# One block of a hybrid encoder on Trainium2: sixteen transfers for the out projection's weight sums, moved and spaced

## The chip, the cores and the metric

The kernel runs on one core of a Trainium2 chip. The metric is device microseconds of one execution, and the time of a kernel is the median over several. A core has five engines that take instructions in order, each from its own queue: TensorE (PE, matmuls; PEld are its weight loads), VectorE (DVE), ScalarE (ACT), GpSimd (POOL) and SyncE (SP, which here only issues transfers). Transfers are issued by SP, POOL and ACT, each on a queue of its own, and carried out by 16 DMA engines that all queues share.

## The reference

One layer of 1024 frames by 1024 channels. A normalised input goes through one projection, and its columns feed three mixers, whose results are gated, projected, summed and sent through an out projection. A gated convolutional feed-forward block follows.

```python
h = _rmsnorm(x, norm_mix_g[l])
z = h @ w_in[l]
(hq, hf, hi, hg, fq, fk, fv, ff, mq, gate_logits) = jnp.split(z, pts, axis=-1)
y_a = _hgrn2_mixer(hq, hf, hi, hg, ...)      # recurrence, 4 heads, 128x128 state, chunkwise
y_b = _fox_mixer(fq, fk, fv, ff, ...)        # forgetting attention, 8 heads of 64, causal
y_c = _memory_mixer(mq, mem_kv, ...)         # attention into 256 memory tokens
gates = jax.nn.sigmoid(gate_logits).reshape(B, T, N_BRANCH, D_MODEL)
merged = (gates[:, :, 0] * (y_a @ w_br_hgrn[l])
          + gates[:, :, 1] * (y_b @ w_br_fox[l])
          + gates[:, :, 2] * (y_c @ w_br_mem[l]))
x = x + merged @ w_out[l]
x = x + _conv_glu_ffn(_rmsnorm(x, norm_ffn_g[l]), w_up, conv_w, conv_b, w_down)
```

The attention works in blocks of 128 queries: logits plus a cumulative log-forget bias, a causal mask, softmax, and the product with the values. `w_out` is 1024 by 1024 in float32.

## The kernel before

Every large product is made of float32 operands split into a rounded part h and a rest l, and costs three matmuls (`mm3`, lines 108 to 112: h by h, h by l, l by h). Large products are also done in seven block products in place of eight (after Strassen and Winograd), for which sums of blocks of both operands are needed. For the out projection the weight sums are made ahead of time, without any compute engine: `out_sums` (lines 922 to 927) is a generator of 16 transfers of 512 KB within DRAM, issued on POOL's queue. Four blocks of the DRAM tile `od` are each first filled by a copy and then added to by an accumulating transfer, each in two halves: od0 is copied from quarter 2 of `w_out`, od1 from quarter 0, od0 is increased by quarter 3, od3 is copied from quarter 1, od1 is increased by od0, od2 is copied from quarter 0, od3 is increased by od1, od2 by quarter 2. `weight_parts` (line 929) is that generator. What it makes is read much later, at the out projection, from 944 us on.

By time the stages are: memory attention, norm and the first projections up to some 330 us; the forgetting attention, some 330 to 700; the recurrence, some 700 to 935; the out projection to some 1060; the feed-forward block to the end.

Attention and recurrence have much less matrix work than they have chains of small steps, so they are woven with other work. `fill` is a generator of steps: the remaining channel-major projections (lines 746 to 870, the tiles `uh`, `ul`, `us`, `ur`, `uo`), and then the three branch projections, whose weights `w_br` come in as chunks `ur` (line 860). `FOX_FILL` and `HGRN_FILL` say how many steps go to each head, and `weave` deals them between the head's own steps. The order of instructions on each engine is then set by a planner, which simulates a timeline and picks by priority (`ahead` gives the mixers' steps more). `tc.issue_after(x)` makes an instruction be queued behind x on its engine. So any edit in these stages can deal the order of all engines anew.

An attention head h (`fox_attn`, line 1014) goes through eight blocks tb of 128 queries. For each block POOL makes the masked bias `nfm` (line 1027); TensorE makes logits from kh and kl, the two parts of the keys (lines 1033, 1034); VectorE adds the bias and takes the maximum; ScalarE takes Exp; POOL normalises `pt` (line 1051). For each pair of blocks TensorE transposes `pt`, ScalarE casts it (`ph`, line 116), and TensorE multiplies by the values `vhl` (lines 1074, 1075, product `po`). The operands of the next head (`fox_load`, lines 999 to 1010: kh, qa and kl in two transfers of 256 KB each, two `nf` of 256 KB, `vhl` of 512 KB) are issued on SP behind the first store `yp` of the head before it.

The recurrence (`hgrn_mix`, line 1122) goes through 4 heads of two halves. Its loads per half are hG, hH, hq, hz and hi. `kE` is transposed (line 1201), copied by ScalarE as `kT` (line 1203) and used at line 1206. `finish` (lines 1101 to 1120) norms a half's result; it is called eight times, and each call takes two transfers from `weight_parts` and queues them on POOL behind its reciprocal root (line 129). `load_y` (line 937) loads a branch operand of 2 MB as `B22l` and `B22h`.

Of the kernel before, what the change touches and what calls it, by code (L numbers as in the profile page):

```python
# [12 lines left out]
ALU = mybir.AluOpType  # L13
AX = mybir.AxisListType

P = 128
# [52 lines left out]
def tile_block(ctx: ExitStack, tc: tile.TileContext, xT, x_rows, memT, mem_rows, vec, fbias, mats, hmask, w_ff, w_tm, w_cm,  # L69
               w_mkv, w_br, w_out, w_up, w_dn, outT):  # L70
    nc = tc.nc
    V, S, G, PE, SP = nc.vector, nc.scalar, nc.gpsimd, nc.tensor, nc.sync
# [7 lines left out]
    def ps_lg():  # L80
        return pz.tile([P, HB], F32, tag="lg", name="lg", bufs=2)

    def ps_tr():
        return pz.tile([P, HB], F32, tag="tr", name="tr", bufs=2)

    def ps_po():
        return pz.tile([P, HB], F32, tag="po", name="po", bufs=1)
# [34 lines left out]
    def split(eng, h, l, src, sub=None):  # L122
        cast(eng, h, src)
        return (sub or V).tensor_sub(l, src, h.bitcast(F32))  # L124

    def rstd_small(out, ss, n):
        w = ss.shape[1]
        V.tensor_scalar(out, ss, 1.0 / n, EPS, ALU.mult, ALU.add)
        return G.tensor_tensor(out, out, mhalf[:, :w], ALU.pow)
# [790 lines left out]
    def out_sums():  # L920

        half = [slice(2 * a, 2 * a + 2) for a in range(2)]
        copy = [(i, w_out[:, a], {}) for i, a in ((0, 2), (1, 0), (3, 1), (2, 0))]
        add = [(i, b, dict(accum_op=ALU.add)) for i, b in ((0, w_out[:, 3]), (1, od[:, 0]), (3, od[:, 1]), (2, w_out[:, 2]))]
        for i, src, how in (copy[0], copy[1], add[0], copy[2], add[1], copy[3], add[2], add[3]):
            for ks in half:
                yield G.dma_start(od[:, i, ks], src[:, ks], **how)

    weight_parts = out_sums()
# [65 lines left out]
    mskf = pf.tile([P, P], F32, tag="mskf", name="mskf")  # L995
# [3 lines left out]
    def fox_load(h):  # L999
        p, a = h // 2, slice(64 * (h % 2), 64 * (h % 2) + 64)  # L1000
        kh, qa, kl = (pf.tile([P, T], F32R, tag=f"{t}{h % 2}", name=f"{t}_{h}") for t in ("kh", "qa", "kl"))
        for t, (u, v) in ((kh, (0, 0)), (qa, (2, 3)), (kl, (1, 1))):
            SP.dma_start(t[0:64, :].bitcast(F32), kqd[p][u // 2][a, u % 2, :])
            SP.dma_start(t[64:128, :].bitcast(F32), kqd[p][v // 2][a, v % 2, :])
        nf = [pf.tile([P, HB], F32, tag="nf", name="nf", bufs=3) for _ in range(2)]
        for n, t in enumerate(nf):
            SP.dma_start(t, negFd[h:h + 1, n * HB:(n + 1) * HB].partition_broadcast(P))
        vhl = pf.tile([P, 8, P], F32R, tag="vhl", name="vhl", bufs=2)
        SP.dma_start(vhl.bitcast(F32), vhd[h // 4][:, :, h % 4, :])
        return kh, kl, qa, vhl, nf  # L1010
# [3 lines left out]
    def fox_attn(h):  # L1014
        p, a = h // 2, slice(64 * (h % 2), 64 * (h % 2) + 64)
        with tc.issue_after(marks["head"].ins) if h else nullcontext():
            kh, kl, qa, vhl, nf = fox_load(h)
        for tp in range(4):
            pts = []
            for j in range(2):  # L1020
                tb = 2 * tp + j
                ns = (tb + 1) * P
                tsl = slice(tb * P, (tb + 1) * P)
                pt = pf.tile([P, T], F32, tag="pt", name="pt", bufs=4)
                st = pf.tile([P, 4], F32, tag="st", name="st", bufs=4)
                nfm = pf.tile([P, P], F32, tag="nfm", name="nfm")
                G.tensor_tensor(nfm, nf[tb // 4][:, tb % 4 * P:tb % 4 * P + P], mskf, ALU.add)
                m = 0
                for s0 in range(0, ns, HB):
                    w = min(HB, ns - s0)  # L1030
                    ps = ps_lg()
                    with tc.issue_after(begun.ins):
                        PE.matmul(ps[:, :w], qa[:, tsl], kh[:, s0:s0 + w], start=True, stop=False)
                    PE.matmul(ps[:, :w], qa[:, tsl], kl[:, s0:s0 + w], start=False, stop=True)

                    d = w - P if s0 + w == ns else w
                    for lo, hi, bias in ((0, d, nf[s0 // HB][:, :d]), (d, w, nfm)):
                        if lo < hi:
                            V.tensor_tensor_reduce(out=pt[:, s0 + lo:s0 + hi], in0=ps[:, lo:hi], in1=bias,
                                                   op0=ALU.add, op1=ALU.max, scale=1.0, scalar=-3e38,  # L1040
                                                   accum_out=st[:, m:m + 1])
                            m += 1
                if m == 3:
                    V.tensor_tensor(st[:, 0:1], st[:, 0:1], st[:, 2:3], ALU.max)
                if m > 1:
                    V.tensor_scalar(st[:, 2:3], st[:, 0:1], st[:, 1:2], -1.0, ALU.max, ALU.mult)  # L1046
                else:
                    V.tensor_scalar(st[:, 2:3], st[:, 0:1], -1.0, None, ALU.mult)
                S.activation(pt[:, :ns], pt[:, :ns], AF.Exp, bias=st[:, 2:3], accum_out=st[:, 3:4])  # L1049
                V.reciprocal(st[:, 3:4], st[:, 3:4])  # L1050
                G.tensor_scalar(pt[:, :ns], pt[:, :ns], st[:, 3:4], 0.0, ALU.mult, ALU.add)  # L1051
                pts.append(pt)
                yield
            po = ps_po()
            for sp in range(tp + 1):
                ptr = ps_tr()
                w = 384 if sp == tp else 512
                for jj in range(2):
                    sb = 2 * sp + jj
                    ssl = slice(sb * P, (sb + 1) * P)  # L1060
                    if sb <= 2 * tp:
                        PE.transpose(ptr[:, jj * 256:jj * 256 + P], pts[0][:, ssl], ident)
                        PE.transpose(ptr[:, jj * 256 + P:jj * 256 + 256], pts[1][:, ssl], ident)
                    else:
                        PE.transpose(ptr[:, 256:384], pts[1][:, ssl], ident)
                ph = pf.tile([P, HB], F32R, tag="ph", name="ph", bufs=2)
                pl = pf.tile([P, HB], F32R, tag="pl", name="pl", bufs=2)
                split(S, ph[:, :w], pl[:, :w], ptr[:, :w])
                for jj in range(2):
                    sb = 2 * sp + jj  # L1070
                    last = sb == 2 * tp + 1
                    o = po[:, P:256] if last else po[:, 0:256]
                    src = slice(256, 384) if last else slice(jj * 256, jj * 256 + 256)
                    PE.matmul(o, vhl[:, sb, :], ph[:, src], start=(sb == 0), stop=False)
                    PE.matmul(o, vhl[:, sb, :], pl[:, src], start=False, stop=last)  # L1075
                yield
            yp = pf.tile([64, 256], F32, tag="yp", name="yp")
            S.copy(yp, po[64:128, :256])
            V.tensor_add(yp, po[0:64, :256], yp)
            stored = SP.dma_start(yd3[1][a, p, tp * 256:(tp + 1) * 256], yp)  # L1080
            if tp == 0:
                marks["head"] = stored
            yield

    for h in range(8):
        weave((ahead(fox_attn(h), AHEAD), FOX_STEPS), (islice(fill, FOX_FILL[h]), FOX_FILL[h]))
# [14 lines left out]
    def finish(h, n, po, gz):  # L1101
        sl = slice(n * HB, (n + 1) * HB)
        o2 = ph.tile([P, 4, P], F32, tag="kE", name="o2", bufs=2)
        rr = ph.tile([P, 4], F32, tag="rr", name="rr", bufs=2)
        S.activation(o2, po.rearrange("p (b v) -> p b v", b=4), AF.Square)
        V.reduce_sum(rr, o2, axis=AX.X)
        marks["last"] = rstd_small(rr, rr, 4 * P)
        with tc.issue_after(marks["last"].ins):
            for _ in range(2):
                next(weight_parts, None)  # L1110
        for b in range(4):
            S.activation(o2[:, b, :], po[:, b * P:(b + 1) * P], AF.Copy, scale=rr[:, b:b + 1])
        ptr = ps_tr()
        for b in range(4):
            PE.transpose(ptr[:, b * P:(b + 1) * P], o2[:, b, :], ident)
        V.scalar_tensor_tensor(out=gz, in0=ptr, scalar=hgc, in1=gz, op0=ALU.mult, op1=ALU.mult)
        if h < 3:
            late.append(partial(SP.dma_start, yd3[0][:, h, sl], gz))
        else:
            y_last.append(gz)  # L1120

    def hgrn_mix(h):
        St = None
        for n in range(2):
# [85 lines left out]
            for b in range(4):  # L1210
# [4 lines left out]
                if n == 0 or b < 3:  # L1215
# [6 lines left out]
                    St = Sn  # L1222

            late.append(partial(finish, h, n, po, gz))
            yield

# [583 lines left out]
```

## Time and profile before

| what | value |
| --- | --- |
| median of 3 runs | 1707.48 us (1705.03 to 1708.06) |
| profiled execution | 1705.12 us |
| its span | 1703.3 us |
| mean granted TensorE clock | 0.995 |
| TensorE busy | 1672.3 us (98%) |
| VectorE busy | 1222.6 us (72%) |
| ScalarE busy | 844.1 us (50%) |
| GpSimd busy | 441.0 us (26%) |
| the 16 transfers of line 927 | issued from 746.4 to 931.1 us |

The span runs from the first to the last event of the profiled execution; the rest of its time lies around it. Busy times leave out the issuing of transfers. A row of the timeline is start, duration, engine, line, operation, output and inputs, sizes, and in brackets how long the engine sat idle before it and what ended that. TensorE's matmuls are pipelined, so each row's duration overlaps the next one's start. A row of waits is the waiting engine, tile and line, what it waited for, then the total, the number of times and the longest, in us.

### The profile page before, as it was taken

How to read it: one execution, taken by the hardware profiler on the slowest of the kernel's cores; microseconds unless marked ns; L12 is line 12 of the kernel's file. 1: busy time of each engine (PE TensorE's matmuls, PEld its weight loads, DVE VectorE, ACT ScalarE, POOL GpSimd, SP SyncE). 2: the span in 40 equal slices, each digit the busy share in tenths (PEclk: the TensorE clock that was granted, in tenths of full speed). 3: DMA queues.
4: the chain of work that ended last, by engine and by line, in shares of the span. 5: the costliest groups of instructions: out<-in, count | busy, mean ns of one | idle time of the engine just before them, and what ended most of it. 6: DMA issues, size and time to landing. Idle time of an engine off the chain costs nothing.

```text
span 1703.3 us, 24929 instructions
## 1 busy us (share of the span) xinstructions
PE 1672.3 (98%) x8883; PEld 1412.6 (83%) x8883; DVE 1222.6 (72%) x2187; ACT 844.1 (50%) x1449; POOL 441.0 (26%) x472
## 2 busy tenths in 40 slices
PE   8999999999999999999999999999999999999999
PEld 5989999777878888888788888888888888788887
DVE  7865766588877666688677768778778777674654
ACT  7745554466656566555333367434444334343331
POOL 1433644565444434222011123211111111100000
PEclk9999999999999999999999999999999999999999
DMA  7353453855545452547756996755345454394772
GB/s 288 111 187 108 162 211 102 256 178 184 187 116 162 146 158 88 185 157 259 265 167 167 273 233 157 226 151 160 117 130 155 130 147 138 139 387 129 263 249 87
DMA packets 133309, 302.92 MB, mean 178 GB/s; under 512 B 14168, under 2 KB 31832, under 8 KB 132544
## 3 DMA queue, kind: packets, MB, share of 16 engines
q1 hardware_dynamic: 101008, 210.87, 36.8%
q0 software_dynamic: 22960, 75.77, 17.6%
q10 hardware_dynamic: 9216, 14.68, 2.4%
q8 instruction: 70, 1.15, 0.3%
q14 instruction: 55, 0.45, 0.1%
HBM read 223.21 MB, written 107.41 MB: 194 GB/s over the span
## 4 chain that ended last, share of the span: by engine, by line
PE 77%; DMA 8%; DVE 7%; issue 4%; ACT 2%; POOL 2%; SPq 1%; DVEq 0%; POOLq 0%; ACTq 0%
PE pp L110 15%; PE pp L112 15%; PE pp L111 15%; PE lg L111 4%; PE lg L112 4%; PE lg L110 4%; PE tr L112 2%; PE tr L110 2%; PE tr L111 2%; DMA hgd<-uo 1%; PE po L110 1%; PE po L112 1%; PE po L1075 1%; PE po L111 1%; DMA fk<-hgd 1%
## 5 line engine op out<-in xcount | busy, mean ns | idle before, releaser
L1349 ACT CAST wh<-s 128x512 fp32r<-128x512 f32 x80 | 48.8, 618 | 119.8 <-PE pp L111 64.8
L116 ACT CAST dwh<-wr 128x1024 fp32r<-128x1024 f32 (+1 forms) x41 | 40.1, 977 | 119.6 <-PE tr L111 40.4
L1349 ACT CAST wh<-rw 128x512 fp32r<-128x512 f32 x70 | 43.0, 620 | 89.3 <-PE pp L111 48.4
L746 ACT CAST uh<-ur 128x512 fp32r<-128x512 f32 x78 | 47.9, 615 | 56.3 <-PE pp L111 40.8
L1472 POOL DMA_DIRECT2D rw<-in_w_up x40 | 22.2, 566 | 199.2 <-DVE wl L1350 162.9
L124 DVE TENSOR_TENSOR dwl<-wr,dwh 128x1024 fp32r<-128x1024 f32 (+1 forms) x41 | 46.3, 1130 | 38.0 <-ACT dwh L116 37.2
L747 DVE TENSOR_TENSOR ul<-us,uh 128x512 fp32r<-128x512 f32 x72 | 55.5, 777 | 24.6 <-ACT uh L746 24.4
L1051 POOL TENSOR_SCALAR pt<-pt,st 128x128 f32<-128x128 f32 (+3 forms) x64 | 56.9, 890 | 56.8 <-DVE st L1050 45.1
L752 POOL TENSOR_TENSOR us<-ur 128x512 f32<-128x512 f32 x36 | 49.0, 1360 | 83.6 <-DMA ur<-in_w_cm 66.6
L747 DVE TENSOR_TENSOR ul<-ur,uh 128x512 fp32r<-128x512 f32 x78 | 61.5, 789 | 12.7 <-ACT uh L746 12.5
L110 PE MATMUL pp<-T2h,uh 128*128 128x512 f32 x168 | 67.3, 403 | 0.2 <-ACT ue L757 0.2
L110 PE MATMUL pp<-B21h,uh 128*128 128x512 f32 x168 | 67.3, 401 | 0.1
L111 PE MATMUL pp<-T2l,uh 128*128 128x512 f32 x168 | 67.0, 399 | 0.0
L112 PE MATMUL pp<-T2h,ul 128*128 128x512 f32 x168 | 66.6, 397 | 0.0
L112 PE MATMUL pp<-B21h,ul 128*128 128x512 f32 x168 | 66.3, 395 | 0.2 <-DVE ul L747 0.2
L111 PE MATMUL pp<-B21l,uh 128*128 128x512 f32 x168 | 66.2, 394 | 0.0
L1049 ACT ACTIVATE pt<-pt,st 128x128 f32<-128x128 f32 (+3 forms) x64 | 49.6, 776 | 30.2 <-DVE st L1046 27.6
L1350 DVE TENSOR_TENSOR wl<-rw,wh 128x512 fp32r<-128x512 f32 x70 | 47.0, 686 | 20.3 <-PE pp L112 16.1
L746 ACT CAST uh<-us 128x512 fp32r<-128x512 f32 x72 | 43.6, 617 | 32.3 <-PE pp L111 21.7
L752 POOL TENSOR_TENSOR us<-us,ur 128x512 f32<-128x512 f32 x36 | 47.6, 1323 | 37.0 <-issue 28.6
L124 DVE TENSOR_TENSOR pl<-tr,ph 128x512 fp32r<-128x512 f32 (+1 forms) x80 | 49.6, 629 | 10.5 <-ACT ph L116 10.0
L1350 DVE TENSOR_TENSOR wl<-s,wh 128x512 fp32r<-128x512 f32 x80 | 54.6, 683 | 0.0
(721 smaller groups left out, 6144.5 us busy)
## 6 DMA issues: line engine op xcount, KB each, us to landing
rw<-in_w_up POOLq DMA_DIRECT2D x40, 512.0 KB, 4.8
ur<-in_w_cm SPq DMA_DIRECT2D x72, 256.0 KB, 3.5
sd<-in_w_dn POOLq DMA_DIRECT2D x30, 512.0 KB, 6.0
br<-yd SPq DMA_DIRECT2D x30, 512.0 KB, 4.3
gd<-uo ACTq DMA_DIRECT2D x48, 256.0 KB, 2.8
gt<-gd SPq DMA_DIRECT2D x48, 256.0 KB, 3.6
yd<-fc SPq DMA_DIRECT2D x44, 256.0 KB, 2.1
raw<-in_w_tm SPq DMA_DIRECT2D x20, 512.0 KB, 4.6
```

The costliest lines, as they stand in the source:

```text
L110: PE.matmul(ps, lh, rh, start=first, stop=False, skip_group_check=more)
L111: PE.matmul(ps, lh, rl, start=False, stop=False, skip_group_check=more)
L112: return PE.matmul(ps, ll, rh, start=False, stop=last, skip_group_check=more)
L116: S.copy(out, in_)
L124: return (sub or V).tensor_sub(l, src, h.bitcast(F32))
L746: marks["cast"] = S.copy(h, src)
L747: V.tensor_sub(l, src, h.bitcast(F32))
L752: G.tensor_add(t, a, b)
L1049: S.activation(pt[:, :ns], pt[:, :ns], AF.Exp, bias=st[:, 2:3], accum_out=st[:, 3:4])
L1051: G.tensor_scalar(pt[:, :ns], pt[:, :ns], st[:, 3:4], 0.0, ALU.mult, ALU.add)
L1349: late["cast"] = S.copy(h, src)
L1350: late["split"] = V.tensor_sub(l, src, h.bitcast(F32))
```

## The change

The sixteen transfers stay as they are and keep their sequence. They are handed out at other places: each of the eight attention heads takes one at block tb = 6, queued on POOL behind that block's masked bias, and each of the eight calls of `finish` takes one in place of two. So the three first steps of the list and the copy of od3 go out in the attention, the rest in the recurrence.

```diff
-                G.tensor_tensor(nfm, nf[tb // 4][:, tb % 4 * P:tb % 4 * P + P], mskf, ALU.add)
+                masked = G.tensor_tensor(nfm, nf[tb // 4][:, tb % 4 * P:tb % 4 * P + P], mskf, ALU.add)
+                if tb == 6:
+                    with tc.issue_after(masked.ins):
+                        next(weight_parts, None)
                 m = 0
...
         marks["last"] = rstd_small(rr, rr, 4 * P)
         with tc.issue_after(marks["last"].ins):
-            for _ in range(2):
-                next(weight_parts, None)
+            next(weight_parts, None)
         for b in range(4):
```

Lines behind the first edit have other numbers in the kernel after: 1051 is 1054 there, 1080 is 1083, and lines 1129 and 1131 are 1131 and 1133. The order of the queues changes from the first attention heads to the end of the recurrence. Three places show it.

On POOL, head 1 around its block 6; `pt` with 768 columns is the softmax of block 5 and with 896 that of block 6. Before:

```order
L1051 TENSOR_SCALAR pt<-pt,st 128x640
L1027 TENSOR_TENSOR nfm<-nf,mskf 128x128
L791 TENSOR_SCALAR uo<-uo 128x512
L792 DMA hgd_80<-uo 128x512
L1051 TENSOR_SCALAR pt<-pt,st 128x768
```

And now:

```order
L1054 TENSOR_SCALAR pt<-pt,st 128x640
L791 TENSOR_SCALAR uo<-uo 128x512
L1027 TENSOR_TENSOR nfm<-nf,mskf 128x128
L927 DMA od<-in_w_out 128x1024
L792 DMA hgd_80<-uo 128x512
L1054 TENSOR_SCALAR pt<-pt,st 128x768
```

The transfer stands behind the bias of block 6, and a store and the normalising of block 5 stand behind the transfer; the clamp of `uo` has moved ahead of the bias.

On SP, around the loads of head 3 (kh_3 to vhl); `fk` and `uo` are results of the projection in the fill that are stored to the recurrence's inputs `hgd3`. Before:

```order
L1009 DMA vhl_4975<-vhd0_74 128x8x128
L966 DMA hgd3_81<-fk_3_6485 128x1024 x2
L812 DMA ur_6868<-in_w_cm 128x512
L1080 DMA yd1_88<-yp_4715 64x256
L799 DMA hgd3_81<-uo_6602 128x512
L799 DMA hgd3_81<-uo_6690 128x512
```

And now:

```order
L966 DMA hgd3_81<-fk_3_6492 128x1024
L812 DMA ur_6876<-in_w_cm 128x512
L1083 DMA yd1_88<-yp_4640 64x256
L1003 DMA kh_3_4965<-kqd1_71 64x1024
...
L1009 DMA vhl_4978<-vhd0_74 128x8x128
L966 DMA hgd3_81<-fk_3_6492 128x1024
L799 DMA hgd3_81<-uo_6609 128x512
L1083 DMA yd1_88<-yp_4717 64x256
L799 DMA hgd3_81<-uo_6697 128x512
```

One of the two stores of `fk` and the load of `ur` have moved from behind the head's loads to ahead of them.

On SP in the recurrence, around the fourth chunk of a branch weight (ur_9553 before, ur_9556 now) and the 2 MB of B22. Before:

```order
L860 DMA ur_9500<-in_w_br 128x512
L888 DMA gt_9392<-gd_86 128x512
L1131 DMA hi_2_9188<-hid1_77 128x4x128
L888 DMA gt_9390<-gd_86 128x512
L1129 DMA hG_3_9587<-hgd3_81 128x512
L1129 DMA hH_3_9588<-hgd3_81 128x512
L888 DMA gt_9498<-gd_86 128x512
L937 DMA B22l_9387<-yd2_89 128x2048
L937 DMA B22h_9386<-yd2_89 128x2048
L1129 DMA hq_3_9589<-hgd3_81 128x512
L860 DMA ur_9553<-in_w_br 128x512
```

And now:

```order
L1133 DMA hi_2_9192<-hid1_77 128x4x128
L860 DMA ur_9556<-in_w_br 128x512
L937 DMA B22l_9390<-yd2_89 128x2048
L937 DMA B22h_9389<-yd2_89 128x2048
L888 DMA gt_9443<-gd_86 128x512
L860 DMA ur_9619<-in_w_br 128x512
L888 DMA gt_9499<-gd_86 128x512
L1131 DMA hG_3_9590<-hgd3_81 128x512
L1131 DMA hH_3_9591<-hgd3_81 128x512
```

The chunk has moved ahead of the 2 MB, and the last head's hG and hH behind them.

## The prediction

> **What bounds the kernel now.** I read the page's busy times first, then windows by stage, then TensorE's waits between 330 and 950 us, then the timeline around the longest of them.
>
> ```profile
> span 1703.3 us, 24929 instructions
> PE 1672.3 (98%) x8883; PEld 1412.6 (83%) x8883; DVE 1222.6 (72%) x2187; ACT 844.1 (50%) x1449; POOL 441.0 (26%) x472
> q1 hardware_dynamic: 101008, 210.87, 36.8%
> q0 software_dynamic: 22960, 75.77, 17.6%
> ...
> 330.00:500.00 170.00, 161.26 (x817) 133.62 (x818) 136.69 (x359) 107.74 (x200) 87.77 (x94) 0.98 0.55 175
> 500.00:700.00 200.00, 200.00 (x1079) 171.03 (x1078) 130.62 (x387) 118.75 (x240) 85.19 (x101) 1.00 0.45 135
> 700.00:950.00 250.00, 245.08 (x1353) 206.18 (x1353) 196.47 (x364) 114.02 (x219) 39.04 (x38) 0.99 0.69 217
> 410.00:420.00 10.00, 6.67 (x27) 5.21 (x26) 6.61 (x18) 5.48 (x10) 4.32 (x5) 0.83 1.03 319
> 470.00:480.00 10.00, 7.15 (x31) 6.05 (x31) 7.91 (x19) 7.39 (x17) 7.34 (x9) 0.83 0.28 85
> 810.00:820.00 10.00, 6.40 (x29) 4.67 (x29) 5.94 (x14) 3.48 (x7) 0.00 (x0) 0.83 1.02 337
> 1100.00:1200.00 100.00, 100.00 (x432) 80.89 (x431) 76.86 (x115) 41.44 (x63) 16.74 (x27) 1.00 0.55 157
> ```
>
> The columns of a window are its length, the busy time of PE, PEld, DVE, ACT and POOL with counts, the granted clock, the DMA share and GB/s. TensorE is busy 98% of the span, so the time is its work plus its gaps. The change touches no matmul and only the stretch from the attention to the end of the recurrence, 330 to 950 us. There TensorE idles 8.7 + 0.0 + 4.9 = 13.7 us. That is all a transfer can give back, besides the slow matmuls behind a gap (the clock of 0.83 in three of the windows). Which waits make it up:
>
> ```profile
> PE tr L1206 <- ACT kT L1203: 3.6, 1, 3.6
> PE lg L1034 <- DMA kl<-kqd: 2.6, 1, 2.6
> PE lg L1033 <- DMA qa<-kqd: 1.5, 2, 0.8
> PE po L1074 <- ACT ph L116: 1.5, 1, 1.5
> PE po L1075 <- DVE pl L124: 1.4, 1, 1.4
> PE tr L1201 <- ACT kE L1193: 0.9, 1, 0.9
> ```
>
> The columns are the total, the number of waits and the longest. Three places matter: the load of attention head 2's operands near 412 us, a hiccup near 470 us, and one wait in the recurrence near 812 us. In two of them, 410 to 420 and 810 to 820, the DMA engines are full (share 1.02 to 1.03). The last one is the one that transfers of `out_sums` take part in:
>
> ```profile
> 797.45 0.32 SPq L937 DMA_DIRECT2D B22l<-yd  x1
> 797.86 0.38 SPq L937 DMA_DIRECT2D B22h<-yd  x1
> 798.81 13.86 DMA ur<-in_w_br
> 801.74 1.76 POOL L927 DMA_DIRECT2D od<-in_w_out  x2
> 812.74 0.62 ACT L746 CAST uh<-ur 128x512 fp32r<-128x512 f32 x1 [8.77 <-DMA ur<-in_w_br]
> 814.28 1.28 PE L1206 MATMUL tr<-hi,kT 128*128 128x128 f32 x6 [3.60 <-ACT kT L1203]
> 816.00 0.69 DVE L1136 TENSOR_TENSOR E<-hG,hH 128x512 f32<-128x512 f32 x1
> 816.21 0.63 PE L112 MATMUL pp<-B21h,ul 128*128 128x512 f32 x1
> 817.49 0.63 PE L112 MATMUL pp<-T2h,ul 128*128 128x512 f32 x1
> ```
>
> (The third row is from the chain of waits: a transfer and how long it took. That chain has it as its longest piece here.) A quarter-MB chunk of a branch weight, issued behind 2 MB of B22 and joined by two transfers of `out_sums`, lands after 13.86 us. ScalarE's cast waits 8.77 us for it; the copy kT is queued behind that cast; TensorE waits 3.6 us for kT.
>
> **The price of one transfer.** q0 is POOL's queue, which carries all of `out_sums`: 17.6% of 1703.3 us is 300 us for 75.77 MB, 3.96 us per MB, so 2.1 us for one transfer of 0.524 MB if the engines have nothing idle. The bounds: at q1's rate (36.8%, 210.87 MB, 2.97 us per MB) it is 1.56 us; in idle engines it is nothing; and the slowest of the present transfers, which go out in pairs, gives
>
> ```profile
> DMA to landing us min/median/max: 4.3/6.6/11.9
> ```
>
> 11.9 / 2 = 6.0 us. I call the price p, take 2.1 because it is the same queue's own mean, and keep 0 to 6.0.
>
> **Term 1 and 2: a copy beside the next head's loads.** Eight transfers now go out at query block 6 of the attention heads, behind the masked bias on POOL. The next head's kh, qa and kl go out on SP at nearly the same moment.
>
> ```profile
> 359.04 0.91 POOL L1027 TENSOR_TENSOR nfm<-nf,mskf 128x128 f32<-128x128 f32 x1
> 359.50 0.60 SPq L1004 DMA_DIRECT2D kl<-kqd  x1
> kl<-kqd SPq DMA_DIRECT2D x2, 256.0 KB, 6.0
> 366.48 0.28 PE L1034 MATMUL lg<-kl,qa 128*128 128x128 f32 x1
> 403.59 0.46 POOL L1027 TENSOR_TENSOR nfm<-nf,mskf 128x128 f32<-128x128 f32 x1 [3.39 <-DVE st L1039]
> 408.02 0.60 SPq L1004 DMA_DIRECT2D kl<-kqd  x1
> 412.52 0.30 PE L1033 MATMUL lg<-kh,qa 128*128 128x128 f32 x1 [0.72 <-DMA qa<-kqd]
> 415.43 0.45 PE L1034 MATMUL lg<-kl,qa 128*128 128x128 f32 x1 [2.61 <-DMA kl<-kqd]
> ```
>
> (The third row is a DMA issue group: size and median time from issue to landing.) For head 1 kl lands at 359.50 + 6.0 = 365.5 and is used at 366.48: 1.0 us to spare. A copy takes that up and costs p − 1.0 = +1.1 us (0 to +5.0). For head 2 kl is late already, by 2.61 us, so the copy counts whole, less what the new order puts in front: between the first product po of the head before and this kl matmul stand matmuls of 28160 columns before and 29440 now. The row 1100 to 1200 gives 100 us for 432 matmuls of 512 columns, 0.452 ns a column, so 1280 columns are 0.6 us. Term 2 is p − 0.6 = +1.5 us (−0.6 to +5.4). Heads 3 to 7 I cost at nothing: from 500 to 700 TensorE has no idle time at all, and its cover there is the projection work that the fill deals between the blocks; with that gone each would cost p. POOL's own time for the issue (0.9 us for one of the two at 801.74) delays the normalising of pt behind it and one store; POOL is 26% busy, so nothing. The accumulating transfers wait on POOL for the copies before them, and the next bias and pt would be queued behind such a wait; but the heads are 403.59 − 359.04 = 44.6 us apart and the slowest landing is 11.9, so none waits.
>
> **Term 3: the hiccup at 470.**
>
> ```profile
> 453.93 0.46 POOL L1027 TENSOR_TENSOR nfm<-nf,mskf 128x128 f32<-128x128 f32 x1 [6.07 <-DVE st L1039]
> 462.76 3.24 SPq L799 DMA_DIRECT2D hgd<-uo  x2
> 470.40 0.63 ACT L797 ACTIVATE uo<-ue 128x512 f32<-128x512 f32 x1 [3.55 <-DMA hgd<-uo]
> 470.94 1.05 ACT L116 CAST ph<-tr 128x512 fp32r<-128x512 f32 x2
> ```
>
> ScalarE waits 3.55 us for a store to free its buffer uo; the cast ph is behind it; TensorE waits 1.5 + 1.4 us, and the matmuls after it run slow. How slow is seen best behind the other gap: 816.21 to 817.49 is three steps of 0.43 us where a 512-column matmul takes 100/432 = 0.23, and the timeline has seven such in a row, 1.4 us. So 2.9 + 1.4 = 4.3 us hang here. In the new order on SP 0.52 MB of fk and 0.26 MB of ur are issued before head 3's loads instead of between them and these stores: at q1's rate 2.3 us earlier. Against it stands the new copy at 453.93, p = 2.1 later. And the waiting instruction stands two casts later on ScalarE, one row of 1.05 us. Together −2.3 + 2.1 − 1.05 = −1.3 us (−4.3, when it is gone, to +2.6, when the copy costs 6.0).
>
> **Term 4: the wait at 812.** In the new order the fourth branch chunk is issued ahead of B22l and B22h, and one transfer goes out in place of two at 801.74. Issued at B22l's place, 797.45, with kl's slower time from issue to landing in a full burst (2.61 us late at 415.43 from 408.02: 7.4 us), it lands at 804.9. ScalarE began to wait at 812.74 − 8.77 = 803.97, and TensorE only at 814.28 − 3.60 = 810.68, so the wait is covered. 3.6 + 1.4 = 5.0 us hang here. But hG and hH of the last head's second half now go out behind the 2 MB, and VectorE wants them at 816.00 − 5.0 = 811.0. From 797.45 to their end 3.7 MB of loads and one transfer are to be moved, 4.2 MB, 12.4 us at the 337 GB/s of the row 810 to 820, so near 810 plus what is still under way: only just in time. I take −4.5 us (−5.0 to 0).
>
> **Term 5: the wait for kE near 711.** Between the last matmul of the attention and this transpose stand 25728 columns before and 27264 now: 0.7 us more cover of the 0.9 us waited. −0.7 us (−0.9 to 0).
>
> The order of all engines is dealt anew between the first heads and the end of the recurrence. The 13.7 us of idle time less the 11.5 us listed leave small waits of 2.2 us which may move either way; 0.
>
> **The sum:** 1.1 + 1.5 − 1.3 − 4.5 − 0.7 = −3.9 us; in p it is 3p − 10.2. The profiled execution took 1705.12 us (span 1703.3 plus 1.8 around it), so 1701.2; it lies 2.4 below the median of the runs, 1707.48, so the forecast is 1703.6 us. With p from 1.56 (q1's price) to 3.3 (half the median pair landing of 6.6) it runs from 1702.0 to 1707.2.
>
> On p there is a rule too. The Trainium skill, DMA: Bandwidth & Descriptors, section Specifications, gives some 358 GB/s as the HBM limit of one core. A copy from DRAM to DRAM reads and writes, 1.05 MB, an estimated 2.9 us by that page; the sum by it would be −1.5 us, 1706.0. The bursts here stay under that limit (319 and 337 GB/s), so the trace does not contradict the rule, and the queue's mean decides for the sum.
>
> **The rivals.** A: the copies are hidden. If the bursts end in idle engines soon enough, p is 0 and the sum is 0 − 0.6 − 3.4 − 4.5 − 0.7 = −9.2, 1698.3 us. For it: the DMA share is only 0.55 and 0.45 over the attention. Against it: it is 1.03 exactly where the copies go.
>
> B: the stall at 812 only changes its name. hG and hH behind the 2 MB hold VectorE, ScalarE's Exp and the next logits as long as the branch chunk did, or the order on ScalarE leaves kT behind another late cast. Term 4 is 0 and the sum +0.6, 1708.1 us: no change that can be told. For it: the bytes in the burst are mostly B22's, which nobody removes. Against it: half of the stage's transfers are gone.
>
> C, on the other side: a copy holds up the next head's loads by more than its mean price, since the 2 MB of those loads and it are in the queues at once and the head cannot start without all of kl. Place: heads 1 to 3. The time is over 0.2% slower from 3p − 10.2 = +3.4, that is p = 4.5 us. At the upper price of 6.0 it is +7.8, 1715.3 us. For it: the pair landing of 11.9 us in a burst. Against it: POOL's mean price is under half of the threshold.
>
> That the change does nothing of what it says is excluded by the order of the instructions; that the transfers as such never cost anything (nobody waited for od, and the 812 wait is B22's alone) is B.
>
> **How the numbers follow.** Forecast 0.45, A 0.17, B 0.20, C 0.18. A measurement of this kernel tells 0.2%, 3.4 us, from no change: faster is below 1704.1, slower above 1710.9. The forecast lies just below that edge: 0.25 faster, 0.20 the same. A is faster. Of B 0.14 is the same and 0.06 slower, since a moved stall can also be longer than the old one. C is slower. That makes 0.42 faster, 0.34 the same, 0.24 slower. The range goes from 1698.0 (A) to 1712.0, a little over half the way from B to C; the forecast's own is 1702 to 1707.
>
> **What would show it.** Right: TensorE's waits after no longer have L1206 on kT at 3.6 us, the wait for kl of head 2 has grown from 2.6 to some 4 us and head 1 has one of about 1, the transfers land in 5 to 8 us, and from 500 to 700 TensorE stays without idle time. Rival A would show kl's wait no longer than now. B would show a new wait of 3 us or more between 800 and 830, on hG, E or a cast. C would show waits of 5 us or more for kl at heads 1 to 3, or idle time at heads 4 to 7. Wrong altogether would be a change of TensorE's busy time after 950 us, where the order is the same.

## The result: slower, and the profile after

The changed kernel takes 1713.61 us (median of 6 runs, 1708.22 to 1717.41) against 1706.91 for the kernel before: a ratio of 1.0037 with a 95% interval of 1.0023 to 1.0051, 0.37% slower. The forecast was 1703.6, and the range ended at 1712.0.

The profiled execution took 1712.49 us, 7.4 more than the one before. Its page begins (the last row is POOL's queue):

```profile
span 1710.7 us, 24942 instructions
PE 1673.2 (98%) x8883; PEld 1410.7 (82%) x8883; DVE 1218.2 (71%) x2187; ACT 842.4 (49%) x1449; POOL 441.9 (26%) x472
...
q0 software_dynamic: 22960, 75.77, 18.0%
```

TensorE's work is the same, so the difference is gaps. The windows by stage (length, then busy time of PE, PEld, DVE, ACT and POOL, then clock, DMA share, GB/s), first of the changed kernel:

```profile
0.00:330.00 330.00, 314.74 (x2387) 295.42 (x2388) 219.14 (x348) 187.39 (x348) 134.56 (x104) 0.99 0.52 172
330.00:500.00 170.00, 159.47 (x792) 130.22 (x791) 130.79 (x343) 104.16 (x190) 88.80 (x94) 0.98 0.59 186
500.00:700.00 200.00, 197.19 (x1066) 168.24 (x1065) 132.63 (x397) 117.13 (x240) 88.78 (x107) 1.00 0.50 146
700.00:950.00 250.00, 246.28 (x1372) 206.73 (x1372) 189.29 (x359) 112.66 (x222) 38.04 (x32) 1.00 0.61 189
810.00:820.00 10.00, 9.44 (x50) 7.60 (x50) 9.09 (x21) 5.94 (x14) 3.02 (x2) 1.00 0.97 348
```

and the one stage of the kernel before that was not shown:

```profile
0.00:330.00 330.00, 317.51 (x2402) 296.96 (x2403) 222.56 (x350) 188.30 (x349) 138.19 (x106) 0.99 0.53 173
```

Idle time of TensorE in the attention (330 to 700) rose from 8.7 to 10.5 + 2.8 = 13.3 us. In the recurrence (700 to 950) it fell from 4.9 to 3.7, and the window from 810 to 820, which had 3.6 us idle, has 0.6. The 2.8 us that are missing before 330 us lie ahead of the first moved transfer, which goes out at 362.8 us, in a stage whose instructions are the same; I take them for the spread from one execution to the next and for no effect of the change. Up to 363 us TensorE's order is the same in both kernels, and there the changed kernel's matmuls are 2.9 us behind already; so of the 7.4 us between these two traces some 3 are spread, and the medians decide on the size. The waits of TensorE between 330 and 950 us of the changed kernel (total, times, longest):

```profile
PE lg L1037 <- DMA kl<-kqd: 5.0, 4, 1.5
PE lg L1036 <- DVE st L1042: 2.7, 1, 2.7
PE pp L110 <- ACT ue L757: 2.5, 4, 1.2
PE pp L110 <- ACT uh L746: 2.0, 1, 2.0
PE pp L110 <- DVE uo L138: 1.4, 1, 1.4
PE tr L1066 <- POOL pt L1054: 1.0, 1, 1.0
```

The wait for kT is gone, as forecast. In its place stand waits for kl, which is late at four heads (2, 3, 5 and 6) where it was late at one (2) before, and five kinds of small waits for casts, sums and softmax. Head 5, which did not wait before, shows how kl comes to be late. These are rows of the changed kernel's timeline and of its DMA issues (size, median time to landing):

```profile
554.84 0.87 POOL L927 DMA_DIRECT2D od<-in_w_out  x1
555.25 0.55 SPq L1003 DMA_DIRECT2D kh<-kqd  x1
558.53 0.66 SPq L1004 DMA_DIRECT2D kl<-kqd  x1
568.82 0.33 PE L1037 MATMUL lg<-kl,qa 128*128 128x128 f32 x1 [1.29 <-DMA kl<-kqd]
...
od<-in_w_out POOLq DMA_DIRECT2D x1, 512.0 KB, 8.8
kl<-kqd SPq DMA_DIRECT2D x2, 256.0 KB, 10.3
```

The same loads of head 5 in the kernel before:

```profile
kl<-kqd SPq DMA_DIRECT2D x2, 256.0 KB, 7.0
```

The transfer goes out 0.4 us ahead of the head's first load, and kl takes 3.3 us longer. That is more than the cover of this head: between the landing of kl and its use stood 2.5 us in the kernel before.

### The profile page after: what moved, and what is told of

Its sections match the earlier page's. It is cut to its first block, busy times and chain, and to the rows that moved or that the text cites. A ratio compares the mean times of both kernels' runs of the same rounds, so it can differ in the third digit from the quotient of the medians.

```text
span 1710.7 us, 24942 instructions
## 1 busy us (share of the span) xinstructions
PE 1673.2 (98%) x8883; PEld 1410.7 (82%) x8883; DVE 1218.2 (71%) x2187; ACT 842.4 (49%) x1449; POOL 441.9 (26%) x472
## 4 chain that ended last, share of the span: by engine, by line
PE 77%; DMA 8%; DVE 7%; ACT 3%; issue 3%; POOL 1%; SPq 1%; ACTq 0%; DVEq 0%; POOLq 0%
PE pp L110 15%; PE pp L111 15%; PE pp L112 15%; PE lg L112 4%; PE lg L111 4%; PE lg L110 4%; PE tr L110 3%; PE tr L112 3%; PE tr L111 3%; DMA kl<-kqd 2%; DMA kqd<-ko 1%; PE po L110 1%; PE po L111 1%; PE po L112 1%; DMA hgd<-uo 1%
## 5 line engine op out<-in xcount | busy, mean ns | idle before, releaser
L124 DVE TENSOR_TENSOR dwl<-wr,dwh 128x1024 fp32r<-128x1024 f32 (+1 forms) x41 | 46.3, 1129 | 41.0 <-ACT dwh L116 41.0
L1027 POOL TENSOR_TENSOR nfm<-nf,mskf 128x128 f32<-128x128 f32 x64 | 35.6, 556 | 82.6 <-DVE st L1042 49.6
```

## Experiments

Two things changed at once: the places of the transfers, and the order that the planner gave to all engines. Most runs therefore take the order from a table: an edge without a semaphore from each instruction to the one that is to follow it on its engine, so that only the transfers move. In the diffs `sums_behind(x, n)` queues the next n of the sixteen transfers behind x; each diff is against a kernel in the same held order, with the transfers at the places of before or at those of the change.

```diff
+        for places in held.values():
+            row = [own[k] for k in places]
+            for a, b in zip(row, row[1:]):
+                tc.add_manual_dep(b, a.name, mybir.DependencyInfo(
+                    mybir.DependencyClass.NoSync, mybir.DependencyReason.DATA), reason="hold")
```

"Old order" is that of the kernel before, "new order" that of the changed kernel. Ratios are to the kernel before, run on the same chip, with their 95% intervals; 0.1% is 1.7 us. A ratio is an estimate from all runs of both kernels and can differ by 0.1% from the quotient of their medians. Theory P: the places cost the time. Its rival O: the new order costs it.

**The new order alone.** The new order, with the transfers where they were.

```diff
-                if tb == 6:
-                    sums_behind(masked, 1)
...
-        sums_behind(marks["last"], 1)
+        sums_behind(marks["last"], 2)
```

> Every engine keeps the order that the change gave it, but the sixteen transfers go out where they were before, two behind each of the eight reciprocal roots of the recurrence; none goes out in the attention. Theory P (place: the transfers beside the next head's loads cost the time): the waits for kl, 5.0 us in the changed kernel, fall to at most the 2.6 us of before, the wait for the branch chunk near 812 stays away, and the time is 1703 to 1707 us, level with the kernel before or up to 4 us faster. Theory O (order: the new order of all engines costs it, whatever the transfers do): 1711 to 1715 us, as in the changed kernel, with the waits for uh near 388, for st near 464 and for uo near 727 still there.

Measured: 1705.22 us, ratio 0.9983 (0.9973 to 0.9993), somewhat faster than before. Its waits, and head 5's loads of kl:

```profile
PE lg L1069 <- DVE st L1075: 2.7, 1, 2.7
PE pp L139 <- ACT uh L775: 2.0, 1, 2.0
PE pp L139 <- DVE uo L167: 1.1, 1, 1.1
...
PE lg L1070 <- DMA kl<-kqd: 0.3, 1, 0.3
...
kl<-kqd SPq DMA_DIRECT2D x2, 256.0 KB, 7.4
```

The waits for st, uh and uo are the new order's, and it gains all the same. Theory O falls in the form that it has here: the new order does not cost the time by itself. With eight of the transfers moved into the attention this order loses 1.0037 − 0.9983 = 0.54%, 9 us.

**The places alone.** The old order, with the transfers where the change puts them.

```diff
-        sums_behind(marks["last"], 2)
+        sums_behind(marks["last"], 1)
...
+                if tb == 6:
+                    sums_behind(masked, 1)
```

> Every engine keeps the order of the kernel before; only the sixteen transfers are moved as in the change, one behind the masked bias of block 6 of each attention head and one behind each reciprocal root. Theory P: waits for kl at three or more heads, together 5 us or more, the 3.6 us for kT near 812 smaller by at most 2 us, and 1711 to 1715 us. Theory O: no new waits over 1 us, 1705 to 1708 us.

Measured: 1710.52 us, ratio 1.0009 (0.9997 to 1.0022): not clear of no change, between the two expectations and nearer to that of P. So the places alone do not show the loss of the change either; it comes with the places and the new order together. The trace is plainer than the time:

```profile
PE lg L1072 <- DMA kl<-kqd: 5.6, 4, 2.6
PE po L1112 <- ACT ph L145: 2.8, 1, 2.8
...
PE tr L1242 <- ACT kT L1239: 0.9, 1, 0.9
...
kl<-kqd SPq DMA_DIRECT2D x2, 256.0 KB, 10.2
```

kl is waited for at heads 1, 2, 4 and 5, 5.6 us in place of 2.6, and the wait for kT falls from 3.6 to 0.9 without any load of the chunk having moved. From a head's first load to the landing of kl it takes 10.7, 11.5, 12.2, 10.9, 13.4, 11.2 and 10.6 us at heads 1 to 7, where the kernel before has 9.1, 10.4, 9.9, 10.1, 10.1, 8.4 and 9.2, in the same order of instructions: 1.9 us more on average, between 0.8 and 3.3. The eight transfers less in the recurrence take away 2.7 of the 3.6 us for kT, more than the 2 us that Theory P allowed, and the eight in the attention give it back. This explains in part why the two changes do not add up (−0.17% and +0.09% alone, +0.37% together): in the new order no wait for kT is left that fewer transfers in the recurrence could shorten.

**Block 3 for block 6, old order.**

```diff
-                if tb == 6:
+                if tb == 3:
```

> As the run before, every engine in the order of the kernel before, but the attention's transfers stand behind the bias of block 3, some 12 to 20 us ahead of the next head's loads, where the DMA share of the kernel before is 0.2 to 0.4. Theory P: no wait for kl beyond those of before; 1704 to 1707 us, 5 us or more under the run with block 6. Theory O: the same time as the run with block 6 within 2 us.

Measured: 1705.44 us, ratio 0.9985 (0.9970 to 0.9999): 0.24% better than with block 6, and as Theory P expected. In one order, with the same number of transfers in each stage, the place within the head matters.

**No transfers, old order.** No `sums_behind` is left, and the out projection reads other blocks.

```diff
...
-    weights = (w_out[:, 0], w_out[:, 1], od[:, 0], od[:, 1], od[:, 3], od[:, 2], w_out[:, 3])
+    weights = (w_out[:, 0], w_out[:, 1], w_out[:, 2], w_out[:, 1], w_out[:, 3], w_out[:, 2], w_out[:, 3])
```

> The order of the kernel before, without the sixteen transfers: the out projection reads parts of w_out where it would read the sums, so the sums are left out. If the transfers take part in the wait near 812 (the forecast's term 4 had half of it from them), the 3.6 us for kT fall below 1.5 and the time is 1702 to 1704 us. If that wait is the work of the 2 MB of B22 alone (rival B), kT is still waited for 2.5 us or more and the time is 1705 to 1708 us.

Measured: 1703.48 us, ratio 0.9966 (0.9953 to 0.9979), and no wait for kT is left. So the 2 MB of B22 alone do not make the stall at 812, and with that the ground of the prediction's rival B falls. Its sign, a new wait of 3 us or more between 800 and 830, is not in the changed kernel either: the longest there is 1.2 us, for ue at 802. In the kernel before the sixteen transfers cost 0.34%, 5.8 us.

**Block 3, new order.** The diff is the one above, in the new order.

> The change with one number other: every engine in the changed kernel's order, one transfer per reciprocal root in the recurrence, but the attention's transfers stand behind the bias of block 3 in place of block 6. If the place beside the loads is the cause, the kl waits (5.0 us in the changed kernel, 0.3 with the transfers out of the attention) stay under 1.5 us and the time is 1702 to 1706 us. If any transfer in the attention costs as much in this order, 1711 us or more.

Measured: 1707.88 us, ratio 1.0009 (0.9997 to 1.0020), above the expected 1706 and 0.28% better than with block 6. The kl waits are 1.6 us, just over the 1.5 expected. The transfers away from the loads still cost 0.26% against the run with none of them in the attention (0.9983). So the place beside the loads explains about half of what this order loses to the eight transfers in the attention. The remainder is spread over small waits and was not traced to one of them; the largest growth is in the waits for ue, 5.5 us here against 3.1 with no transfer in the attention.

**On the loads' own queue.** One copy behind vhl on SP for each of heads 1 to 7, in the new order; the last copy and all accumulating transfers in the recurrence.

```diff
-        SP.dma_start(vhl.bitcast(F32), vhd[h // 4][:, :, h % 4, :])
+        values = SP.dma_start(vhl.bitcast(F32), vhd[h // 4][:, :, h % 4, :])
+        if h:
+            sums_behind(values, 1)
...
```

> The changed kernel's order; one transfer a head still goes out within the burst of the next head's loads, but on the loads' own queue, SP, directly behind vhl, for heads 1 to 7 (copies only, the accumulating ones all go to the recurrence, one per reciprocal root and two at the first). If the price comes from POOL's queue taking a share of the engines from loads already queued on SP, kl lands within 10.5 us of a head's first load again, as with no transfer there (8.4 to 10.5), kl waits stay under 1.5 us, and the time is 1703 to 1708 us. If half a MB more in the burst costs the same on any queue, kl lands after 11.5 us or more at several heads and the time is 1710 us or more.

Measured: 1709.92 us, ratio 1.0017 (1.0007 to 1.0026). Head 5's loads of kl:

```profile
kl<-kqd SPq DMA_DIRECT2D x2, 256.0 KB, 6.4
```

kl lands 8.8 to 10.5 us after a head's first load again, and its waits fall to 0.6 us. So a copy behind the loads on their own queue leaves them alone. The run changes two things, though, the queue and the moment: at head 5 this copy goes out at 558.3 us, 6.0 us behind the head's first load and 1.9 behind the last issue of kl, where the change has it 0.4 us ahead of the first load. The Trainium skill, DMA: Bandwidth & Descriptors, section Queues, rings and completion order, says that each DMA engine takes turns between the queues that have work for it, packet by packet. The 10.3 us of kl with the copy on POOL's queue and the 6.4 with it on SP's agree with that, but they would also agree if the moment alone counted. At head 1 of the changed kernel the copy stands on POOL's queue and goes out 0.4 us behind the last issue of kl, and kl takes 6.2 us there, against 7.1 without a copy. What the queue itself does is therefore not shown. The time was higher than the first expectation. TensorE waits longer for st (4.2 us against 2.7 in the run with the new order alone), for ue (4.3 against 3.1) and for pt (2.3 against 0.9); that loads queued behind the copy are the cause is likely, but was not traced.

**All sixteen in the attention, old order**, behind the biases of blocks 3 and 4.

```diff
-                if tb == 6:
+                if tb in (3, 4):
...
-        sums_behind(marks["last"], 1)
```

> The order of the kernel before, all sixteen transfers in the attention, behind the biases of blocks 3 and 4, none in the recurrence. If what is left of the wait for kT near 812 comes from the transfers of the recurrence, it falls from 0.6 us (one per root) to about 0 and the time is 1702 to 1706 us, close to the run without the sums (1703.5). If two per head reach the next loads, kl waits exceed 3 us and it is 1707 us or more.

Measured: 1713.12 us, ratio 1.0029 (1.0019 to 1.0040). The time is that of the second expectation, but not for its reason: kl is waited for 2.5 us, no more than before. Of the losses the trace shows one whole: the loads `ur` of the fill are late. The first row is POOL's waits of this run from 330 to 700 us, the second a piece of its chain of waits:

```profile
POOL us L781 <- DMA ur<-in_w_cm: 45.1, 11, 7.3
...
664.66 8.57 DMA ur<-in_w_cm
```

In the kernel before the same waits are

```profile
POOL us L752 <- DMA ur<-in_w_cm: 26.1, 9, 6.6
...
ur<-in_w_cm SPq DMA_DIRECT2D x72, 256.0 KB, 3.5
```

A load of 256 KB, 3.5 us in the median, takes 8.57 beside two transfers (issued at 662.5 and 663.9 us). The sum of weight blocks waits for it on POOL, the bias and the softmax stand behind that sum, and TensorE waits 2.2 us for the softmax. That is one of several losses: TensorE falls 11 us behind the kernel before between 330 and 725 us, and its waits of 2.4 us for ue and 1.9 us for VectorE's yp were not traced. The attention's DMA share of some 0.5 was not room for all sixteen.

**Block 3, planner free.** The changed kernel with one number other.

```diff
-                if tb == 6:
+                if tb == 3:
```

> The changed kernel with block 3 for block 6 and nothing else; the planner deals all orders by itself. If the place decides, no kl waits over 3 us together and 1703 to 1708 us. If a newly dealt order costs as much by itself, 1710 us or more with waits for casts and sums.

Measured: 1708.71 us, ratio 1.0010 (0.9999 to 1.0020), just over the first expectation. kl is waited for 1.3 us in all, and new waits for casts (uh 3.2 and 2.3 us) have come with the newly dealt order.

**No transfers, new order.** The edit of the run without transfers, in the new order.

> The changed kernel's order without the sixteen transfers: the out projection reads parts of w_out where it would read the sums, so the sums are left out. It is the floor for the three runs in this order that carry them. If the new order is better by itself, 1699 to 1702 us, under the run without sums in the old order (1703.5). If its gain was only that it hides the transfers of the recurrence better, 1702.5 to 1705 us. If the waits that the new order made for casts and sums cost more than it gains, 1706 us or more.

Measured: 1701.79 us, ratio 0.9971 (0.9958 to 0.9983). The time alone lies in the band for a better order, but the kernel before was also faster in this comparison (1706.84 against 1707.57), and by the ratios both orders take the same without transfers (0.9966 and 0.9971). So neither is shown to be better by itself. All sixteen in the recurrence cost 0.12% over this floor in the new order and 0.34% in the old one; at the change's places they cost 0.66% and 0.43%. With intervals of some 0.13% on each ratio the first of these differences is barely clear of noise and the second is not.

**A sixteenth of the bytes, at the change's places, new order.**

```diff
-                yield G.dma_start(od[:, i, ks], src[:, ks], **how)
+                yield G.dma_start(od[:8, i, ks], src[:8, ks], **how)
...
```

> The changed kernel's order with all sixteen transfers at the change's places, each of 8 of 128 partitions, so a sixteenth of the bytes; the out projection reads parts of w_out where it would read the sums, so the sums are left out. If the bytes in the DMA engines are what costs, the time is within 2 us of the run without transfers in this order, and kl waits are under 1 us. If POOL's time for the issue and what it holds up there (the normalising, the sums us) costs, 1709 us or more.

Measured: 1702.41 us, ratio 0.9970 (0.9960 to 0.9980), the same as with no transfer at all. The kl waits:

```profile
PE lg L1072 <- DMA kl<-kqd: 0.8, 1, 0.8
```

POOL issues all sixteen at the same places, in the same 0.6 to 0.9 us each, and nothing is lost. So the cost goes with what the transfers move through the DMA engines, and POOL's time for the issue costs nothing that can be measured here.

**Early places, old order**, between 60 and 240 us.

```diff
+EARLY = (6, 6, 6, 7, 7, 9, 11, 19, 21, 21, 25, 25, 27, 29, 67, 67)
...
     weight_parts = out_sums()
+    for at in EARLY:
+        OD_AT.append((next(weight_parts).ins.name, at))
```

(The numbers are places in POOL's order.)

> The order of the kernel before, the sixteen transfers behind sixteen early instructions of POOL between 60 and 240 us, where the DMA share of the kernel before is 0.0 to 0.5; none in the attention or the recurrence. If the place is what counts and these windows have slack, it equals the run without the sums, 1702 to 1705 us. If transfers delay loads that are waited for in any stage, 1707 us or more, with new waits before 330 us.

Measured: 1711.41 us, ratio 1.0022 (1.0009 to 1.0035), as in the second expectation. A wait of TensorE before 330 us, and the piece of the chain behind it:

```profile
PE tr L728 <- POOL mpt L720: 5.2, 3, 4.8
...
238.74 10.05 DMA raw<-in_w_tm
```

In the kernel before the same load takes

```profile
raw<-in_w_tm SPq DMA_DIRECT2D x1, 512.0 KB, 3.2
```

The last pair of transfers went out beside this load, at 236.5 and 237.1 us, and it took 10.05 us. POOL's sum of it stands ahead of the normalising of mpt, which TensorE waits for. TensorE is 0.9 us behind the kernel before in the 1800th matmul, at 245 us, and 7.3 us in the 1900th. One load costs 6 us.

**Early places, new order.** The same edit.

> The same early places in the changed kernel's order. If the early windows have slack, within 1.5 us of the run without transfers in this order; if that is 1699 to 1702 us, this is the fastest of all and beats both kernels. If not, 1706 us or more.

Measured: 1708.61 us, ratio 1.0010 (1.0001 to 1.0018), as in the second of the two; the load raw takes 8.6 us and the wait for mpt is 3.3 us here.

**Early places without that pair, new order.** Eight copies between 68 and 82 us, the accumulating ones from 85 to 160 us.

```diff
-EARLY = (6, 6, 6, 7, 7, 9, 11, 19, 21, 21, 25, 25, 27, 29, 67, 67)
+EARLY = (6, 6, 6, 6, 6, 7, 7, 7, 9, 11, 21, 21, 25, 25, 27, 29)
...
-        for i, src, how in (copy[0], copy[1], add[0], copy[2], add[1], copy[3], add[2], add[3]):
+        for i, src, how in (copy[0], copy[1], copy[2], copy[3], add[0], add[1], add[2], add[3]):
```

> As the run with the early places in the changed kernel's order, but the last pair, which stood beside a load raw near 237 us that then took 10.05 us, goes out before 160 us, where no load is at hand; eight copies go out between 69 and 90 us, where the DMA share of the kernel before is 0.0 to 0.3. If only the nearness of a load that is waited for costs, the 3 to 5 us wait for mpt near 240 is gone and the time is 1701 to 1704 us. If any half MB costs anywhere, it stays at 1706 us or more.

Measured: 1703.76 us, ratio 0.9978 (0.9965 to 0.9990), the lowest ratio of the versions that compute the reference, though not clear of three others (0.9983 to 0.9986). The wait for mpt is gone.

**The same places, old order.**

> The same places in the order of the kernel before. If nearness to a waited load is the cause: 1703 to 1706 us, near the run without the sums in this order (1703.5), and 5 us or more under the first early run. If any half MB costs anywhere: 1708 us or more.

Measured: 1705.62 us, ratio 0.9986 (0.9976 to 0.9997), against 1.0022 with that pair at 237 us. Moving two of sixteen transfers away from one load, and the others somewhat, is worth 0.36%. So bytes do not cost the same anywhere: in the places tried here the price was paid where a load that is waited for was in the engines at the same time.

The runs with a held order in one table, as ratios to the kernel before:

| places of the sixteen | old order | new order |
| --- | --- | --- |
| none | 0.9966 | 0.9971 |
| at the change's places, a sixteenth of the bytes | | 0.9970 |
| early, away from waited loads | 0.9986 | 0.9978 |
| early, one pair beside a load raw | 1.0022 | 1.0010 |
| recurrence, two per root | 1 (the kernel before) | 0.9983 |
| attention block 3 and recurrence | 0.9985 | 1.0009 |
| on SP behind vhl, and recurrence | | 1.0017 |
| attention block 6 and recurrence | 1.0009 | 1.0037 (the change) |
| attention blocks 3 and 4 | 1.0029 | |

## Why the prediction was wrong

**The step that failed** is one sentence of terms 1 and 2: "Heads 3 to 7 I cost at nothing: from 500 to 700 TensorE has no idle time at all". That TensorE did not idle there says that kl was in time, not by how much. In the trace of before the slack, from the landing of kl to its use, is 0.1 us at head 4, 2.5 at head 5 (landing 553.1, use 555.67) and some 4 or more at heads 3, 6 and 7; I did not set it beside the price. The 0.1 is no slack, since the same step stands at head 2, which waits. In the old order this list tells who waits once the transfers are moved: the heads with the least, 2 and 4, 1 (1.0 us) and 5. In the changed kernel the new order has dealt the slack anew, and heads 3, 5 and 6 wait, 0.7 + 1.3 + 1.5 = 3.5 us. The matmuls after each wait are slow for a while, and the stretch from 500 to 700 us has 2.8 us of idle time, which the prediction named as a sign of rival C. Rival C had the mechanism, in too few heads and with a threshold of 4.5 us that was not needed. The forecast missed by 10 us (1713.6 against 1703.6). These three waits, some 4.7 us with the slow matmuls after them, are about half of that; the rest is in the gains of terms 3 to 5 that did not come or were cancelled, and in small waits.

**The price p** came out near: 2.1 us forecast, and kl landed 1.9 us later on average. The two are different quantities, the engines' time for a transfer and the delay of a load, so that they agree may be luck. The estimate of 2.9 by the HBM limit in the Trainium skill, DMA: Bandwidth & Descriptors, section Specifications, was further off. The trace of before does not keep to that limit of 358 GB/s either: its page has a slice of 43 us at 387 GB/s, which the prediction's two windows of 10 us did not show. But the single delays run from 0.8 to 3.3 us in the old order, and in the new one to 3.0 and 3.7 at heads 5 and 6, and a wait is made by the large ones.

**Terms 1 and 2** for themselves: head 1, forecast at +1.1, has no wait in the changed kernel, where its transfer goes out behind the issue of kl, and head 2, forecast at 2.6 + 1.5 = 4.1 us, has 1.5. The new order gave head 2 more cover than the 0.6 us I counted: without a transfer there it would wait 0.3.

**Term 3** named the right waits and they are gone, but other waits came near them, for ue at 458 and st at 464 us. They stand in the run with the new order alone too (ue 0.6 and st 2.7 us), and cancel the gain. I had the small waits of a newly dealt order at 0 in sum.

**Term 4** was right in direction: kT is no longer waited for. I gave the chunk's place on SP most of it, and that suffices: with the new order and all sixteen transfers in the recurrence the wait is gone too. It is not the only way, since with the old order and half the transfers 2.7 of the 3.6 us are gone. The stage did not keep the gain: waits of 1.4 us for uo and 1.2 for ue came in (1.1 and 0.4 with the new order alone), and idle time fell by 1.2 us where terms 4 and 5 together had 3.6 + 0.7 = 4.3 of it.

**The cost that I did not list** is that of the other loads on the same queue. I looked for what is late next only at kh, qa and kl. POOL's sums wait for ur and POOL's biases for nf, and the next softmax is behind both. In the run with all transfers in the attention it is ur: POOL waits 45.1 us for it, where the kernel before has 26.1. In the changed kernel it is nf more than ur: POOL waits 30.0 us for nf and 41.7 for ur, where the run with the new order alone has 16.6 and 38.3. How much of that reaches TensorE was not measured. What does reach it there is mostly kl: by the starts of the matmuls the changed kernel falls 7.6 us behind the run with the new order alone between the first moved transfer and 960 us, and some 6 of them come at the four waits for kl, the slow matmuls after each included.

Two forecasts held: nothing is lost after 950 us (the matmuls of the changed kernel are 8.7 us behind those of the kernel before at 962 us and 7.4 at the end), and POOL's time costs nothing (the run with a sixteenth of the bytes).

## What to carry to other kernels

A DMA share of one half was no sign of room here. What a background transfer cost depended on how early the loads beside it had been issued before their use, so list the slack of each load (landing to first use) and set it beside the largest delay, not the mean. A stage without idle time says that cover was enough, not how much was left. When a change moves transfers and a planner deals the order anew, hold the order and move the transfers alone, then the other way. The two effects need not add up: here they were −0.17% and +0.09% alone and +0.37% together.

## What the runs showed of the hardware that I had not expected

One load can be delayed by more than the engines' time for the transfers beside it: 512 KB beside two transfers took 10.05 us where the same load took 3.2 before, 6.9 more for transfers of an estimated 2.1 us each (POOL's queue mean in the prediction). And a copy in the burst of a head's loads is harmless to them if it goes out late enough: 0.4 us ahead of head 5's loads, on POOL's queue, it delayed kl from 7.4 us (the new order without it) to 10.3; behind them, on SP's queue, kl took 6.4. Whether the queue or the moment does this was not separated.
